# The residual stream of a two-layer decoder kept in feature-major layout: weights become the stationary operand of the second FFN product and the output projection

## The chip, the cores and the metric

The kernel runs on one core of a Trainium2 chip, as one launch. The time is device microseconds of one execution on that core. Before the change the median of three runs is 1272.65 us (1272.11 to 1273.28).

## The reference

Two layers of a decoder trunk over 256 tokens of 1024 features, all in float32. With `rms_norm` over the features, each layer does

```
x = x + 0.5 * swiglu_ffn(x, ffn1_norm, ffn1_wi, ffn1_wo)     # D_FF = 2816
h = rms_norm(x, mix_norm);  parts = split(h @ w_in)          # projections for three attentions and gates
y = g0*(o_sb @ proj_sb) + g1*(o_mla @ proj_mla) + g2*(o_nsa @ proj_nsa)
x = x + y @ w_out
x = x + 0.5 * swiglu_ffn(x, ffn2_norm, ffn2_wi, ffn2_wo)

swiglu_ffn(x, g, wi, wo): a, b = split(rms_norm(x, g) @ wi);  return (silu(a) * b) @ wo
```

The three attentions (stick-breaking, a latent one and a sparse one) are not touched by the change.

## The kernel before

Every product of float32 operands is made as three matmuls: an operand is split into a rounded part (hi) and the rest (lo), and `mm3` adds hi\*hi, hi\*lo and lo\*hi in PSUM. The weights come as a stream of slabs of 128 x 1024 (some smaller). `slab_parts` loads a slab in two halves into `raw` (six buffers, SP's queue), ScalarE (ACT) rounds a half into the hi tile and VectorE (DVE) subtracts to get the lo tile. Slabs live in one of two rings of four: `whi`/`wlo`, or `vhi`/`vlo`, which belong to the pool of a feed-forward block (FFN); `slab_tiles` chooses by the slab's number in its FFN (0 to 65). `next_slab` keeps two slabs ahead of the one in use. TensorE (PE) runs in the program's order; on the other engines a scheduler sets the order, and in the mixer (the attention part) a planner does (`Planner`, with thread after thread of `yield use_...`), for DVE and ACT as well.

The 256 tokens are two tiles of 128 (`t`), and `hq` = `hThi`/`hTlo` hold the normed input with features on the partitions, as the products need it. An FFN goes:

- Chunk 0 (slabs 0 to 3), tokens on the output's partitions: the stationary operand is a tile of `hT`, the moving one 512 columns of a slab, 48 matmuls. Its outputs are transposed by `flush` (four transposes of `g`).
- Chunks 1 to 5 (slabs 4 to 43), in `chunk_T`: the stationary operand is a 128 x 128 piece of a slab, the moving one all 256 tokens of `hq`, 24 matmuls of 256 columns for a slab. The outputs arrive with features on the partitions. `gate_T` multiplies by `rows`, the tokens' norm factors along a row; `spread_rn` makes `rows` once in an FFN by two transposes of `rnb`. The ring of a slab is v, but for slab 6 (slab 8 in the first FFN), which is w.
- The second product (slabs 44 to 65, ring w), in `out_rows`: the stationary operand is a tile of the gated values `gT` (`gh`/`gl`), the moving one 512 columns of a slab, 12 matmuls for a slab. The sums arrive with tokens on the partitions. The last three slabs (`TAIL`) are held together, so that a block of sums is finished while PE does the next.

The end of `out_rows`, for each token tile and half: the residual `x` gets the sums (L674), is multiplied by the next norm's gains (`norm`, L625, gains broadcast over the partitions by a DMA), squared and summed (`norm_scale`), transposed by PE (`half_T`, L612; in the mixer L1064) and split into `hThi` and `hTlo`. The projection `w_out` at the mixer's end is also an `out_rows`, with `yT` as the stationary operand and ring w.

In the text a slab pair of PE rows such as `acc<-hThi,vhi` names output, moving and stationary operand (moving first).

Of the kernel before, what the change touches and what calls it, by code (L numbers as in the profile page):

```python
# [10 lines left out]
F = mybir.dt.float32  # L11
# [348 lines left out]

EARLY_AT = ((27, 29, 31, 33, 35, 37, 39, 41, 43, 45), (28, 26, 32, 34, 36, 38, 40, 42, 44, 48))
# [7 lines left out]
def decoder_trunk(ctx, tc, x_in, xt_in, wts, gains, lcon, cst, out, depth=DEPTH):  # L369
# [42 lines left out]
    def load_x(t, cols=(0, 1)):  # L412
        for c in cols:
            cs = slice(c * 512, (c + 1) * 512)
            nc.sync.dma_start(xs[t][:, cs], x_in[t * 128:(t + 1) * 128, cs])

# [28 lines left out]
    nc.vector.memset(mh, -0.5)  # L445

    gain_q = []

    def load_gain():

        i = gain_n[0]
        gain_n[0] += 1
        if i < 3 * depth:
            g = cp.tile([128, D], F, tag="gain", name="gain", bufs=1)
            nc.sync.dma_start(g, gains[i:i + 1, :].to_broadcast([128, D]))
            gain_q.append(g)

    gain_n = [0]
# [148 lines left out]
    def half_T(src, half):  # L607

        tp = tp_tile()
        for j in range(4):  # L610
            k = half * 4 + j
            nc.tensor.transpose(tp[:, j * 128:(j + 1) * 128], src[:, k * 128:(k + 1) * 128], ident)  # L612
        return tp

    def to_T(dst, src, halves=(0, 1)):

        for half in halves:
            tp = half_T(src, half)
            k = slice(half * 4, half * 4 + 4)
            split(dst[0][:, k, :], dst[1][:, k, :], tp.rearrange("p (a b) -> p a b", a=4))  # L620


    def norm(h, t, c, gain):
        cs = slice(c * 512, (c + 1) * 512)
        nc.vector.tensor_tensor(h[:, cs], xs[t][:, cs], gain[:, cs], op=OP.mult)  # L625

    def norm_scale(t):

        sq = att_tile()
        ss = sm.tile([128, 16], F, tag="ss", name="ss")  # L630
        for c in range(2):
            nc.scalar.activation(sq, xs[t][:, c * 512:(c + 1) * 512], AF.Square, accum_out=ss[:, c:c + 1])
        nc.vector.tensor_scalar(ss[:, 0:1], ss[:, 0:1], ss[:, 1:2], None, op0=OP.add)
        r = rstd(ss, 1.0 / D)
        q = hp.tile([128, 8], F, tag="rn", name="rn", bufs=4)
        for i, m in enumerate((1.0, 0.5, 0.125)):
            nc.vector.tensor_scalar(q[:, i:i + 1], r[:, 0:1], m, None, op0=OP.mult)
        return q

    def enter():  # L640

        return [big_tile("h") for _ in range(NT)], new_T(), [None] * NT
# [8 lines left out]
    def out_rows(lhs, kts, between=None, last=False, by=None):  # L651
# [7 lines left out]
        for k in range(kts - TAIL):  # L659
# [4 lines left out]
            if between is not None:  # L664
                between(k)
        sls = [next_slab() for _ in range(TAIL)]
        if not last:
            gain = gain_q.pop(0)
            nxt[0] = hs, hq, rn = enter()
            hT = of_t(hq)  # L670

        def finish(t, c):
            xv = xs[t][:, c * 512:(c + 1) * 512]
            nc.vector.scalar_tensor_tensor(xv, accs[t, c], by[t][:, 1:2] if by else 0.5, xv, op0=OP.mult, op1=OP.add)  # L674
            if last:
                nc.sync.dma_start(out[t * 128:(t + 1) * 128, c * 512:(c + 1) * 512], xv)
            else:
                norm(hs[t], t, c, gain)

        tail = range(kts - TAIL, kts)  # L680
        for t in range(NT):
            cmajor = last or t == 0
            order = [(k, c) for k in tail for c in range(2)]
            if cmajor:
                order.sort(key=lambda kc: kc[1])
            for k, c in order:
                run(t, c, k, sls[k - tail[0]])
                if t == 1 and not last and c == 0 and k - tail[0] in (0, 1):
                    to_T(hT[0], hs[0], (k - tail[0],))
                if cmajor and k == kts - 1:  # L690
                    finish(t, c)
            if not cmajor:
                for c in range(2):
                    finish(t, c)
            if not last:
                rn[t] = norm_scale(t)


    def ffn(l, gi):
        first = l == 0 and gi == 0  # L700
        if first:
            nxt[0] = hs, hq, rn = enter()
            gain_n[0] = 1
        else:
            hs, hq, rn = nxt[0]
        hT = of_t(hq)
        with ExitStack() as es:
# [8 lines left out]
            gT = [(gq[0][:, :, t, :], gq[1][:, :, t, :]) for t in range(NT)]  # L716
            todo = []
            ahead = split_early(fp, l, 0) if gi == 0 else split_early(fp, l + 1, 1) if l + 1 < depth else iter(())

            def glu(t, a, b, f0, fn):  # L720
                s = fp.tile([128, 512], F, tag="gate", name="sil")
                nc.scalar.activation(s[:, :fn], a[:, :fn], AF.Silu, scale=rn[t][:, 0:1])
                g = fp.tile([128, 512], F, tag="g", name="g")
                nc.vector.tensor_tensor(g[:, :fn], b[:, :fn], s[:, :fn], op=OP.mult)
                todo.append((t, g, f0, fn))

            def flush():
                if todo:
                    t, g, f0, fn = todo.pop(0)
                    tp = tp_tile()  # L730
                    q = fn // 128
                    for j in range(q):
                        nc.tensor.transpose(tp[:, j * 128:(j + 1) * 128], g[:, j * 128:(j + 1) * 128], ident)
                    k0 = f0 // 128
                    split(gT[t][0][:, k0:k0 + q, :], gT[t][1][:, k0:k0 + q, :],
                          tp[:, :fn].rearrange("p (a b) -> p a b", a=q))

            def spread_rn():
# [7 lines left out]
                nc.scalar.activation(rows.rearrange("p t n -> p (t n)"), tp[:, 0:S], AF.Copy)  # L746

            def chunk_T(n, evac):
# [3 lines left out]
                for s in range(KT // g):  # L752
                    sl = next_slab()
                    for b, a in enumerate(accs):
# [9 lines left out]
                        if s == KT // g - 1:  # L764
                            evac(b, a)
                        yield

            def gate_T(b, a):
                if first and ci == b == 0:
                    spread_rn()  # L770
                s = fp.tile([128, 512], F, tag="gate", name="gate")
                nc.vector.tensor_tensor(s.rearrange("p (c n) -> p c n", c=2), a.rearrange("p (c n) -> p c n", c=2),
                                        rows.rearrange("p t n -> p (t n)")[:, None, :].to_broadcast([128, 2, S]),
                                        op=OP.mult)
                nc.scalar.activation(s, s, AF.Silu)
                gates[b] = s

            def value_T(b, a):
                g = fp.tile([128, 512], F, tag="g", name="g")
                nc.vector.tensor_tensor(g, a, gates[b], op=OP.mult)  # L780
# [1247 lines left out]
```

## Time and profile before

| What | Value |
|---|---|
| median of the runs | 1272.65 us |
| profiled execution, first to last instruction | 1270.3 us |
| what lies around that span, against the median | 2.35 us |
| PE / DVE / ACT / POOL busy | 1258.1 / 917.6 / 784.9 / 106.6 us |
| granted TensorE clock, mean | 0.999 |
| matmuls | 8095 |

The profile gives the span of one execution; its own device time is not listed apart, so the span is set beside the median of the runs. Busy time of PE is the union of overlapping matmuls, whose recorded durations are longer than the distance from one start to the next: for the pace of a stretch, the starts of its first and last row and the number of matmuls between them are used, not the mean duration.

The stages in that execution, by the starts of their first matmuls: FFN 1 of layer 0 from 6.30 us, its second product from 127.86, the mixer from 188.67, its `w_out` from 429.18, FFN 2 from 452.85, its second product from 575.73; layer 1 in the same order, with FFN 1 from 636.54, second product from 759.66, `w_out` from 1059.20.

### The profile page before, as it was taken

The page shows a single profiled execution, that of the slowest core. Times are in us where ns is not written, and L with a number is a line of the kernel's source. Part 1 is how long each engine was busy: PE and PEld are TensorE (multiplying, and loading weights), DVE is VectorE, ACT ScalarE, POOL GpSimd, SP SyncE. Part 2 cuts the span into 40 slices and gives each one's busy share as a digit, 9 for nine tenths or more (in the row PEclk, how much of TensorE's full clock was granted, in tenths as well). Part 3 has the DMA queues.
Part 4 walks back from the last instruction along what each step waited for, and adds up shares of the span by engine and source line. Part 5 has one row for each costly group of instructions (what it writes and reads, how often), then busy time and mean ns, then how long its engine had stood idle before and what let it go on. Part 6 is the DMA issues. An engine that isn't in the chain of part 4 may idle for free.

```text
span 1270.3 us, 23545 instructions
## 1 busy us (share of the span) xinstructions
PE 1258.1 (99%) x8095; PEld 1117.0 (88%) x8095; DVE 917.6 (72%) x1922; ACT 784.9 (62%) x1635; POOL 106.6 (8%) x169
## 2 busy tenths in 40 slices
PE   9999999999999999999999999999999999999998
PEld 8999888888877889998889998888888778899986
DVE  7777667878998676776577676678768887766643
ACT  7556557777877565565455565478757774655542
POOL 0012201110000001112000111011100000000000
PEclk9999999999999999999999999999999999999999
DMA  8789977556645567899677899674786455566653
GB/s 311 271 298 340 336 254 231 168 182 225 191 133 167 173 217 252 274 342 326 223 254 261 292 334 341 197 227 153 255 290 221 141 167 176 176 191 199 216 168 114
DMA packets 151961, 294.98 MB, mean 232 GB/s; under 512 B 17824, under 2 KB 19488, under 8 KB 151840
## 3 DMA queue, kind: packets, MB, share of 16 engines
q1 hardware_dynamic: 141984, 261.48, 63.4%
q0 software_dynamic: 9856, 31.99, 6.8%
q8 instruction: 63, 1.03, 0.3%
q14 instruction: 58, 0.48, 0.1%
HBM read 258.27 MB, written 34.60 MB: 231 GB/s over the span
## 4 chain that ended last, share of the span: by engine, by line
PE 91%; DVE 4%; ACT 2%; issue 1%; DMA 1%; POOL 0%; SPq 0%; DVEq 0%; ACTq 0%
PE acc L588 16%; PE acc L590 16%; PE acc L589 16%; PE acc L763 11%; PE acc L761 11%; PE acc L762 11%; PE tp L1562 1%; DVE x L674 1%; DMA raw<-in_wts 1%; PE att L1914 1%; PE att L1471 1%; PE tp L1590 1%; ACT wf L1521 1%; DVE wlo L536 1%; DVE vlo L536 1%
## 5 line engine op out<-in xcount | busy, mean ns | idle before, releaser
L763 PE MATMUL acc<-hThi,vlo 128*128 128x256 f32 x1248 | 344.8, 276 | 0.0
L761 PE MATMUL acc<-hThi,vhi 128*128 128x256 f32 x1248 | 344.8, 276 | 0.0
L762 PE MATMUL acc<-hTlo,vhi 128*128 128x256 f32 x1248 | 344.7, 276 | 0.0
L535 ACT ACTIVATE vhi<-raw 128x512 fp32r<-128x512 f32 x312 | 182.5, 621 | 105.3 <-PE acc L762 42.5
L536 DVE TENSOR_TENSOR vlo<-raw,vhi 128x512 fp32r<-128x512 f32 x312 | 202.9, 685 | 61.8 <-ACT vhi L535 60.1
L762 PEld LDWEIGHTS acc<-hTlo,vhi 128*128 128x128 f32 x1248 | 234.3, 188 | 0.2
L761 PEld LDWEIGHTS acc<-hThi,vhi 128*128 128x128 f32 x1248 | 234.2, 188 | 0.2
L763 PEld LDWEIGHTS acc<-hThi,vlo 128*128 128x128 f32 x1248 | 234.2, 188 | 0.0
L536 DVE TENSOR_TENSOR wlo<-raw,whi 128x512 fp32r<-128x512 f32 x248 | 160.0, 684 | 85.7 <-ACT whi L535 85.4
L535 ACT ACTIVATE whi<-raw 128x512 fp32r<-128x512 f32 x248 | 142.8, 621 | 103.8 <-PE acc L590 78.1
L588 PE MATMUL acc<-whi,hThi 128*128 128x512 f32 (+2 forms) x480 | 188.9, 394 | 0.7 <-ACT whi L535 0.7
L590 PE MATMUL acc<-whi,hTlo 128*128 128x512 f32 (+2 forms) x480 | 183.9, 383 | 0.1
L589 PE MATMUL acc<-wlo,hThi 128*128 128x512 f32 (+2 forms) x480 | 183.1, 382 | 0.2 <-DVE wlo L536 0.2
L998 DVE TENSOR_TENSOR wlo<-raw,whi 128x512 fp32r<-128x512 f32 x216 | 140.8, 678 | 25.7 <-ACT whi L996 24.5
L996 ACT ACTIVATE whi<-raw 128x512 fp32r<-128x512 f32 x216 | 126.2, 617 | 39.2 <-PE acc L590 22.8
L588 PE MATMUL acc<-whi,gh 128*128 128x512 f32 x352 | 137.5, 391 | 0.0
L590 PE MATMUL acc<-whi,gl 128*128 128x512 f32 x352 | 137.0, 389 | 0.0
L589 PE MATMUL acc<-wlo,gh 128*128 128x512 f32 x352 | 137.0, 389 | 0.0
L590 PEld LDWEIGHTS acc<-whi,hTlo 128*128 128x128 f32 x480 | 90.2, 188 | 18.8 <-DVE ss L594 1.3
L588 PEld LDWEIGHTS acc<-whi,hThi 128*128 128x128 f32 x480 | 90.4, 188 | 16.9 <-ACT whi L535 1.4
L589 PEld LDWEIGHTS acc<-wlo,hThi 128*128 128x128 f32 x480 | 90.5, 188 | 14.3 <-DVE wlo L536 0.5
L554 ACT ACTIVATE ehi<-eraw 128x512 fp32r<-128x512 f32 x60 | 37.9, 631 | 100.5 <-DMA eraw<-in_wts 99.1
(315 smaller groups left out, 1912.9 us busy)
## 6 DMA issues: line engine op xcount, KB each, us to landing
raw<-in_wts SPq DMA_DIRECT2D x764, 256.0 KB, 3.4
eraw<-in_wts SPq DMA_DIRECT2D x60, 256.0 KB, 4.8
early<-ehi POOLq DMA_DIRECT2D x60, 256.0 KB, 3.8
early<-elo POOLq DMA_DIRECT2D x60, 256.0 KB, 4.4
whi<-early SPq DMA_DIRECT2D x60, 256.0 KB, 4.0
wlo<-early SPq DMA_DIRECT2D x60, 256.0 KB, 4.1
gain<-in_gains SPq DMA_DIRECT2D x5, 512.0 KB, 5.3
xd<-x SPq DMA_DIRECT2D x4, 512.0 KB, 3.5
```

The lines of the kernel that those rows point to most:

```text
L535: nc.scalar.activation(hi[:, c:c + m], raw[:, :m], AF.Copy)
L536: nc.vector.tensor_tensor(lo[:, c:c + m], raw[:, :m], hi[:, c:c + m], op=OP.subtract)
L554: nc.scalar.activation(hi, raw, AF.Copy)
L588: nc.tensor.matmul(o, a[0], b[0], start=start, stop=False)
L589: nc.tensor.matmul(o, a[0], b[1], start=False, stop=False)
L590: nc.tensor.matmul(o, a[1], b[0], start=False, stop=stop)
L674: nc.vector.scalar_tensor_tensor(xv, accs[t, c], by[t][:, 1:2] if by else 0.5, xv, op0=OP.mult, op1=OP.add)
L761: nc.tensor.matmul(o, sl[0][:, w], h, start=k == 0 and c == 0, stop=False)
L762: nc.tensor.matmul(o, sl[0][:, w], l_, start=False, stop=False)
L763: nc.tensor.matmul(o, sl[1][:, w], h, start=False, stop=k == KT - 1 and c == 1)
L996: nc.scalar.activation(hl[0][:, c:c + m], raw[:, :m], AF.Copy)
L998: nc.vector.tensor_tensor(hl[1][:, c:c + m], raw[:, :m], hl[0][:, c:c + m], op=OP.subtract)
```

## The change

The residual is kept transposed: `xs` holds features on the partitions, tokens along the row, all the time. The rest follows.

- `out_T` takes the place of `out_rows` for three of the four second products and both `w_out`: stationary is a 128 x 128 piece of a slab, moving are all 256 tokens of `gq` or `yT`, 24 matmuls of 256 columns for a slab where there were 12 of 512. The finish of a block of 256 features (four blocks, `b`): multiply by `rows` into `u` (not for `w_out`), add to `x`, make `hThi`/`hTlo` of two feature tiles with the gain as a scalar per partition (`part_T`, ACT and DVE), square and add up (`add_squares`, ACT and DVE).
- The transposes of `h` and the broadcast gains go. All gains are one tile `gcol`. The sums of squares over the features are two float32 matmuls with a column of ones (`sum_squares`, L617), and `row_scales` makes the factors of both token tiles.
- Chunk 0 is done by a `chunk_T` too (96 matmuls of 256 columns, ring w), and the four transposes of `g` go; what needs `rows` before it is there is kept in `pend` until `spread_rn`. The square sums stand behind its third slab, in the first FFN behind the third slab of chunk 1. In the first FFN `spread_rn` moves from slab 7 to behind slab 9; slab 8 is still the one in ring w.
- The second products' slabs are in ring v, but in the last FFN. The last FFN keeps `out_rows` and so needs `x` with tokens on the partitions: `x_rows`, four times four transposes, one group in each of chunks 2 to 5.
- In the mixer `lat` takes both token tiles for each feature tile, instead of all feature tiles for each token tile, and `yT`, `V0` and `V1` have other layouts.

```diff
+    def part_T(dst, k, v, w):
+        nc.scalar.activation(dst[0][:, k], v, AF.Copy, scale=w)
+        nc.vector.scalar_tensor_tensor(dst[1][:, k], v, w, dst[0][:, k], op0=OP.mult, op1=OP.subtract)
+    def add_squares(sq, b, v):
+        nc.scalar.activation(sq[:, 512:1024] if b else sq[:, 0:512], v, AF.Square)
+        if b:
+            nc.vector.tensor_tensor(sq[:, 0:512], sq[:, 0:512], sq[:, 512:1024], op=OP.add)
+        if b == 3:
+            nc.vector.tensor_tensor(sq[:, 0:S], sq[:, 0:S], sq[:, S:2 * S], op=OP.add)
+    def sum_squares(sq):
+        a = att_tile()
+        for t in range(NT):
+            nc.tensor.matmul(a[:, t:t + 1], sq[:, t * 128:(t + 1) * 128], one, start=True, stop=True)
+        return a
...
+    def out_T(src, kts, gi, between=None, scale=None):
+        accs = [acc_tile() for _ in range(KT // 2)]
+        def run(b, k, sl):
+            h, l_ = src[0][:, k], src[1][:, k]
+            for c in range(2):
+                o = accs[b][:, c * S:(c + 1) * S].rearrange("p (t n) -> p t n", t=NT)
+                w = slice((2 * b + c) * 128, (2 * b + c + 1) * 128)
+                nc.tensor.matmul(o, sl[0][:, w], h, start=k == 0 and c == 0, stop=False)
+                nc.tensor.matmul(o, sl[0][:, w], l_, start=False, stop=False)
+                nc.tensor.matmul(o, sl[1][:, w], h, start=False, stop=k == kts - 1 and c == 1)
...
+        for b in range(KT // 2):
+            for j in range(TAIL):
+                run(b, kts - TAIL + j, sls[j])
+            xv = xs[b // 2][:, b % 2 * 512:b % 2 * 512 + 512]
+            v = accs[b]
+            if scale is not None:
+                v = scale(v)
+            nc.vector.scalar_tensor_tensor(xv, v, 0.5, xv, op0=OP.mult, op1=OP.add)
+            for k in (2 * b, 2 * b + 1):
+                part_T(hq, k, block(k), gcol[:, gi * KT + k:gi * KT + k + 1])
+            add_squares(sq, b, xv)
...
-        if not 4 <= j < FFN_SLABS - DFF // 128 or j == 6 and i != j or i == 8:
+        end = FFN_SLABS - DFF // 128 if i >= len(stream) - FFN_SLABS else FFN_SLABS
+        if not 4 <= j < end or j == 6 and i != j or i == 8:
...
+                drain(chunk_T(512, both), lambda i: scale_cols() if i == 5 else None)
...
             def hook(i):
-                if i == 3 and ci == 0 and not first:
+                if ci == 0 and first:
+                    if i == 5:
+                        scale_cols()
+                elif ci == 0 and i == 3:
                     spread_rn()
-                if i == (7 if first and ci == 0 else 3):
-                    while todo:
-                        flush()
+                if last and ci and i == 3:
+                    x_rows(ci - 1)
+                hook2(i)
+            def first_spread(i):
+                if i == 3:
+                    spread_rn()
                 hook2(i)
```

The built programs hold 8095 and 9203 matmuls. Three places show what moved. The first is PE in the first FFN, around `spread_rn` and `flush`. Before, at slab 7, after which slab 8 (ring w) follows:

```order
L763 MATMUL acc<-hThi,vlo 128x256
L733 MATMUL tp<-ident,g 128x128 x4
L761 MATMUL acc<-hThi,whi 128x256
L762 MATMUL acc<-hTlo,whi 128x256
L763 MATMUL acc<-hThi,wlo 128x256
```

Now, behind slab 9:

```order
L742 MATMUL acc<-hThi,vlo 128x256
L720 MATMUL tp<-ident,rnb 128x128 x2
L740 MATMUL acc<-hThi,vhi 128x256
L741 MATMUL acc<-hTlo,vhi 128x256
L742 MATMUL acc<-hThi,vlo 128x256
```

The transposes of `g` are gone; those of `rnb` are now followed by slabs of ring v alone, to the end of the FFN (816 matmuls with `hq`, then 528 with `gq`).

The second place is PE in chunk 0 of the FFN that follows another FFN (layer 1, FFN 1). Before, transposes of `h` stand between its matmuls:

```order
L590 MATMUL acc<-whi,hTlo 128x512
L612 MATMUL tp<-ident,h 128x128 x4
L588 MATMUL acc<-whi,hThi 128x512
L589 MATMUL acc<-wlo,hThi 128x512
L590 MATMUL acc<-whi,hTlo 128x512
```

Now the two matmuls of the square sums stand there, behind 72 of 96 matmuls:

```order
L742 MATMUL acc<-hThi,wlo 128x256
L617 MATMUL att<-gcol,sq 128x1 x2
L740 MATMUL acc<-hThi,whi 128x256
L741 MATMUL acc<-hTlo,whi 128x256
L742 MATMUL acc<-hThi,wlo 128x256
```

PE waits there for the finished sums of squares, where it waited for the residual times its gain. The third place is DVE at the same boundary. Before, these are the instructions that end with the transposed `h` in `hTlo`:

```order
L674 SCALAR_TENSOR_TENSOR x_5516<-acc_7473,rn_5759,x_5516 128x512
L536 TENSOR_TENSOR wlo_8089<-raw_8090,whi_8088 128x512
L625 TENSOR_TENSOR h_7984<-x_5516,gain_6200 128x512
L536 TENSOR_TENSOR wlo_8089<-raw_8094,whi_8088 128x512
L536 TENSOR_TENSOR vlo_8077<-raw_8098,vhi_8075 128x512
L625 TENSOR_TENSOR h_7984<-x_5516,gain_6200 128x512
```

Now, from behind the last block's residual to the last addition of squares (L611), for which PE's L617 waits (`wlo_8877` is slab 6 of the next FFN, `vlo_8726`, `vlo_8841` and `vlo_8911` are its slabs 4, 5 and 7):

```order
L609 TENSOR_TENSOR sq_8609<-sq_8609 128x512
L525 TENSOR_TENSOR wlo_8877<-raw_8878,whi_8876 128x512
L525 TENSOR_TENSOR wlo_8877<-raw_8882,whi_8876 128x512
L599 SCALAR_TENSOR_TENSOR hTlo_8608<-x_5803,gcol_106,hThi_8607 128x256 x2
L525 TENSOR_TENSOR vlo_8726<-raw_8797,vhi_8724 128x512
L525 TENSOR_TENSOR vlo_8726<-raw_8801,vhi_8724 128x512
L525 TENSOR_TENSOR vlo_8841<-raw_8842,vhi_8840 128x512
L525 TENSOR_TENSOR vlo_8841<-raw_8846,vhi_8840 128x512
L609 TENSOR_TENSOR sq_8609<-sq_8609 128x512
L525 TENSOR_TENSOR vlo_8911<-raw_8912,vhi_8910 128x512
L525 TENSOR_TENSOR vlo_8911<-raw_8916,vhi_8910 128x512
L611 TENSOR_TENSOR sq_8609<-sq_8609 128x256
```

The lo halves of four slabs, which are used after L617, stand ahead of that last addition in DVE's order.

More of the change, by code (lines that the diff above doesn't have):

```diff
@@ L410, in cc @@
         return ct[:p, o:o + w]
[L412 to L415, printed above, removed]
     def warm_up(n):
@@ L445, in decoder_trunk @@
     nc.vector.memset(mh, -0.5)
[L447 to L458, printed above, removed]
+    gcol = cp.tile([128, 128], F, name="gcol")
+    nc.vector.memset(gcol[:, NG:NG + 16], 1.0)
+    one = gcol[:, NG:NG + 1]
     lc_t = [None]
@@ L605, in of_t @@
         return [(q[0][:, :, t, :], q[1][:, :, t, :]) for t in range(NT)]
[L607 to L620, printed above, removed]
@@ L663, in out_rows @@
                     run(t, c, k, sl)
-            if between is not None:
-                between(k)
         sls = [next_slab() for _ in range(TAIL)]
[L667 to L675, printed above, removed]
-                nc.sync.dma_start(out[t * 128:(t + 1) * 128, c * 512:(c + 1) * 512], xv)
[L677 to L696, printed above, removed]
+        for t in range(NT):
+            for c in range(2):
+                for j in range(TAIL):
+                    run(t, c, kts - TAIL + j, sls[j])
+                xv = xo[t][:, c * 512:(c + 1) * 512]
+                nc.vector.scalar_tensor_tensor(xv, accs[t, c], by[t][:, 1:2], xv, op0=OP.mult, op1=OP.add)
+                nc.sync.dma_start(out[t * 128:(t + 1) * 128, c * 512:(c + 1) * 512], xv)
     def ffn(l, gi):
         first = l == 0 and gi == 0
+        last = l == depth - 1 and gi == 2
         if first:
[L702 to L706, printed above, removed]
+            nxt[0] = new_T(), big_tile("sq")
+        hq, sq = nxt[0]
         with ExitStack() as es:
@@ L715, in ffn @@
             own.append((vhi, fp.tile([128, 1024], R, tag="vlo", name="vlo", bufs=W_BUFS)))
-            gT = [(gq[0][:, :, t, :], gq[1][:, :, t, :]) for t in range(NT)]
-            todo = []
+            rn, pend = [None] * NT, []
             ahead = split_early(fp, l, 0) if gi == 0 else split_early(fp, l + 1, 1) if l + 1 < depth else iter(())
[L720 to L736, printed above, removed]
             def spread_rn():
@@ L764, in chunk_T, with soon @@
                         if s == KT // g - 1:
-                            evac(b, a)
+                            soon(evac, b, a)
                         yield
[L768 to L772, printed above, removed]
+            spread, gates = [False], {}
+            def soon(f, *a):
+                if spread[0]:
+                    f(*a)
+                else:
+                    pend.append(lambda: f(*a))
@@ L836, in first_steps @@
+                    part_T(hq, k, v, xt[:, k:k + 1])
+                parts, sl = [], []
+                accs = [acc_tile() for _ in range(2)]
                 with tc.manual_schedule(engines={nc.vector.engine, nc.scalar.engine, nc.sync.engine}):
@@ L902, in between, with scale @@
                     next(ahead, None)
-            out_rows(gT, DFF // 128, between, last=l == depth - 1 and gi == 2, by=rn)
+            if last:
+                out_rows([(gq[0][:, :, t, :], gq[1][:, :, t, :]) for t in range(NT)], DFF // 128, rn, xo)
+            else:
+                def scale(a):
+                    u = fp.tile([128, 512], F, tag="g", name="u")
+                    by_rows(u, a)
+                    return u
+                out_T(gq, DFF // 128, 3 * l + gi + 1, between, scale)
     def mixer(l):
```

239 lines of the change are left out of this document (117 added, 122 removed).

## The prediction

> **What bounds the kernel now.** I read the page from the top: the busy times, the clock, the chain that ended last.
>
> ```profile
> PE 1258.1 (99%) x8095; PEld 1117.0 (88%) x8095; DVE 917.6 (72%) x1922; ACT 784.9 (62%) x1635; POOL 106.6 (8%) x169
> PEclk9999999999999999999999999999999999999999
> PE 91%; DVE 4%; ACT 2%; issue 1%; DMA 1%; POOL 0%; SPq 0%; DVEq 0%; ACTq 0%
> L763 PE MATMUL acc<-hThi,vlo 128*128 128x256 f32 x1248 | 344.8, 276 | 0.0
> L588 PE MATMUL acc<-whi,gh 128*128 128x512 f32 x352 | 137.5, 391 | 0.0
> ```
>
> TensorE bounds everything, at full clock in every slice; only some tens of us are waits. So the question is how long PE takes for the matmuls as they are now cut, and whether it waits at the new seams. The mean durations (276 and 391 ns) overlap and would mislead: two of 256 columns are not 552 ns. The pace comes from the starts in the timeline of PE.
>
> ```profile
> 127.86 0.40 PE L588 MATMUL acc<-whi,gh 128*128 128x512 f32 x1
> 184.33 0.60 PE L612 MATMUL tp<-ident,h 128*128 128x128 f32 x4
> ...
> 17.81 0.28 PE L761 MATMUL acc<-hThi,vhi 128*128 128x256 f32 x1
> 27.71 0.38 PE L745 MATMUL tp<-ident,rnb 128*128 128x128 f32 x2
> 27.84 0.36 PE L761 MATMUL acc<-hThi,vhi 128*128 128x256 f32 x1
> 28.05 0.28 PE L762 MATMUL acc<-hTlo,vhi 128*128 128x256 f32 x1
> 29.35 0.60 PE L733 MATMUL tp<-ident,g 128*128 128x128 f32 x4
> 29.70 0.36 PE L761 MATMUL acc<-hThi,whi 128*128 128x256 f32 x1
> 29.90 0.28 PE L762 MATMUL acc<-hTlo,whi 128*128 128x256 f32 x1
> 32.66 0.28 PE L761 MATMUL acc<-hThi,vhi 128*128 128x256 f32 x1
> ...
> 465.90 0.28 PE L761 MATMUL acc<-hThi,vhi 128*128 128x256 f32 x1
> 471.56 0.38 PE L745 MATMUL tp<-ident,rnb 128*128 128x128 f32 x2
> ```
>
> - 512 columns: 249 matmuls from 127.86 to 184.33, 226.8 ns each.
> - 256 columns with weights in ring w: 23 from 29.90 to 32.66, 120.0 ns.
> - 256 columns with weights in ring v: 840 from 32.66 to 127.86, 113.3 ns. But the same kind took 84 from 17.81 to 27.71, 117.9 ns, and 11 from 28.05 to 29.35, 118.2 ns.
>
> So ring v has two paces. The slow one stands after a start from 512-column matmuls (17.81) and after a start from transposes (28.05); the fast one stands only behind slab 8, which is in ring w (29.70). The other three FFNs repeat it, slow before their slab in ring w (48 from 465.90 to 471.56, 117.9 ns) and fast behind it. In the built program `whi` and `wlo` start a multiple of 512 bytes from the `hT` tiles, `vhi` 192 bytes off such a multiple; the changed program has the same distances, and sets `gh` to `vhi` and `yT` to `whi` 192 off as well.
>
> **The change, part by part.** T is the end of a product on PE. The seams before, and the lat stage:
>
> ```profile
> 6.30 0.50 PE L588 MATMUL acc<-whi,hThi 128*128 128x512 f32 x1 [0.71 <-ACT whi L535]
> ...
> 184.69 0.48 PE L588 MATMUL acc<-whi,gh 128*128 128x512 f32 x1
> 186.16 0.60 PE L612 MATMUL tp<-ident,h 128*128 128x128 f32 x4
> 193.57 0.45 PE L588 MATMUL acc<-whi,hThi 128*128 128x440 f32 x1
> 199.69 0.40 PE L588 MATMUL acc<-whi,hThi 128*128 128x512 f32 x1
> 429.18 0.39 PE L588 MATMUL acc<-whi,yT 128*128 128x512 f32 x1
> 475.09 0.28 PE L761 MATMUL acc<-hThi,vhi 128*128 128x256 f32 x1
> 575.73 0.40 PE L588 MATMUL acc<-whi,gh 128*128 128x512 f32 x1
> 640.34 0.65 PE L612 MATMUL tp<-ident,h 128*128 128x128 f32 x4 [0.91 <-DVE h L625]
> 659.02 0.28 PE L761 MATMUL acc<-hThi,vhi 128*128 128x256 f32 x1
> 759.66 0.40 PE L588 MATMUL acc<-whi,gh 128*128 128x512 f32 x1
> 831.51 0.39 PE L588 MATMUL acc<-whi,hThi 128*128 128x512 f32 x1
> ```
>
> Prices. The change splits 1176 matmuls of 512 into pairs of 256 (3 x 264 in second products, 2 x 96 in `w_out`, 4 x 48 in chunk 0). At the fast pace a pair costs 2 x 113.3 = 226.6 ns: nothing; at the slow one 9 ns more, in ring w with `hT` 13 more. A group of four transposes costs 0.36 us (184.33 to 184.69), and the six matmuls behind it 1.47 us (to 186.16) instead of 1.36: 0.47. Two `rnb` transposes with the restart: 0.3. The float32 square sums (two of one column) appear nowhere; below, two transposes (0.22 us), above, a group of four twice over (0.94); I take 0.5 with the restart, nearer to the transposes because the weights loaded are the same 128 x 128. The lat matmuls take 204 ns (30 from 193.57 to 199.69).
>
> The Trainium skill ("TensorE: Matmul & The Clock Gate", section "Back-to-back issue gap") puts N/2.4 + 2.5 ns on a warm matmul, so 2.5 ns for each of the 1176 that are added: 2.9 us against the change. The trace differs: 256 columns take exactly half of 512 at the fast pace, so no such term stands in the sum.
>
> What DVE must do at a seam:
>
> ```profile
> 639.00 0.68 DVE L536 TENSOR_TENSOR wlo<-raw,whi 128x512 fp32r<-128x512 f32 x1
> 639.60 0.68 DVE L625 TENSOR_TENSOR h<-x,gain 128x512 f32<-128x512 f32 x1
> 640.20 0.68 DVE L536 TENSOR_TENSOR wlo<-raw,whi 128x512 fp32r<-128x512 f32 x1
> ...
> L772 DVE TENSOR_TENSOR gate<-acc,rows 128x512 f32<-128x512 f32 x40 | 27.2, 685 | 9.5 <-PE acc L763 9.5
> L833 DVE SCALAR_TENSOR_TENSOR hTlo<-h,xt,hThi 128x256 fp32r<-128x256 f32 x6 | 2.9, 478 | 0.0
> raw<-in_wts SPq DMA_DIRECT2D x764, 256.0 KB, 3.4
> ```
>
> Back to back, 512 elements cost DVE 0.60 us; 256 elements then cost about 0.39 (478 ns less the same overlap of 85). By the order of the changed kernel, from the first block's sums to the last addition of squares:
> - FFN to FFN: 20 of 512 (4 `u`, 4 residuals, 3 additions, 9 half slabs), 8 `hTlo`, one short addition: 12.0 + 3.1 + 0.3 = 15.4 us. PE allows three blocks of 18 (6.12) and 72 in ring w (8.64), 14.8 us. So PE waits 0.7 us at least; since slab 7 loads into the `raw` buffer that slab 4 frees late (3.4 us to landing), up to 3.5. I take 2.0. Queued behind that wait are slab 3's matmuls and all that follows.
> - `w_out` to FFN: 18 of 512 (no `u`, 11 half slabs): 14.2 us against 6.4 + 8.6. Nothing to 1.5; I take 0.5.
> - FFN to mixer: 14 of 512: 11.8 us against 6.1 + 36 x 0.204 = 13.5. No wait; `lat` by feature tile needs the last ones only at T + 7.3.
>
> The tiles themselves come in time: the last `hTlo` pair stands eight DVE instructions ahead of L611, and is needed by slab 3.
>
> The sum against the trace, with the slow pace after each restart into ring v (us, now minus before):
> 1. First FFN to slab 8, 26.36 (6.30 to 32.66): chunk 0 96 x 0.120 + 0.63 of waits as before, slabs 4 to 6 at the fast pace since they follow ring w 8.16, square sums 0.5, slab 7 2.83, slab 8 2.88: 26.5, +0.2.
> 2. Slabs 9 to 43, 95.20: slab 9 2.72, `rnb` 0.3, then 816 x 0.1179 = 96.2: +4.0. No slab of ring w follows the transposes any more.
> 3. Second product and lat, 71.83 (127.86 to 199.69): 528 x 0.1179 + 48 x 0.204 + 0.6: 72.6, +0.8. (The 16 transposes removed are paid away by the pace.)
> 4. `w_out` to slab 6, twice 45.91 (429.18 to 475.09): 192 x 0.1179, two groups of `y` 0.94, chunk 0 11.52, square sums and wait 1.0, slabs 4 and 5 5.44, `rnb` 0.3, slab 6 2.88: 44.7, -2.4 for both.
> 5. FFN to FFN, 83.29 (575.73 to 659.02), fast since slab 6 is in ring w behind `rnb`: 59.8 + 11.5 + 0.5 + 2.0 + 5.4 + 0.3 + 2.9 = 82.5, -0.8.
> 6. Layer 1 FFN to mixer, 71.85: 59.8 + 9.8 + 0.6 = 70.2, -1.6.
> 7. Last FFN: four groups `x_rows` 1.9, and from the first on 720 matmuls slow (720 x 4.6 ns = 3.3): +5.2.
>
> Together +5.3 before rounding: 1275.6 against the span of 1270.3, and with the 2.35 us around it, as in the median, 1278.0. Costed at nothing: the gain broadcasts that go and the residual's new DMAs (under PE work with two slabs ready); ACT's share of `part_T`, which is shorter than DVE's; the new order at the mixer's start, where only a few groups change places. If that cover is gone, the late one is DVE's weight split, since it already ends waits at these seams.
>
> **Rivals.**
> - *The fast pace holds.* If a restart does not bring the slow pace back, 816 + 528 + 384 + 720 = 2448 matmuls lose their 4.6 ns: 11.3 us less, 1266.7, faster. For it: nowhere before is a fast stretch interrupted, so that it is lost has not been seen. Against it: five clean starts into ring v all ran slow. It decides at a mean pace of 115.7 ns over these 2448. The Trainium skill (same page, "Step-by-step: what each phase is for") says "Loading the next tile's weights doesn't steal SBUF read bandwidth from the running matmul"; by that all should run alike, as here. The trace disagrees already, with 113.3, 117.9 and 120.0 ns for one shape.
> - *Slow only beside `hT`.* If the pace recovers with `gh` or `yT` as moving tile (no row has them), terms 3 and 4 lose 4.2: 1273.8.
> - *DVE is later than counted.* With 3.5 us and twice 1.5 of waits, and a row of `raw` loads behind them: 1281.5. For it: 0.91 us of waiting for DVE at 640.34 already, with less queued. Against it: 640.34 is DVE work that PE needs at once, the new tiles have 5 to 7 us.
>
> **Chances.** Slow pace after restarts 0.50, fast pace 0.27, slow beside `hT` alone 0.15, late DVE 0.08. A change under 0.2% (2.5 us) can't be told from none here. Faster is the second case and a little of the third, 0.29; the same, most of the third and the edge of the first, 0.16; slower 0.55. The range 1266 to 1282 takes in the second and the last case; the first alone has 1275 to 1281.
>
> **What would show it.** In the timeline after: `acc<-gh,vhi` of layer 0's FFN 1 at 118 ns and of its FFN 2 at 113; chunk 0 at 120; a wait of PE at L617 with DVE as releaser, longest between the layers; no row L612 of `h`; DVE not above 75%. The prediction is wrong if the paces of those two second products are equal, or if PE waits several us in the mixer.

## The result, and the profile after

The changed kernel takes 1286.13 us (median of 4 executions, 1284.61 to 1287.78), the kernel before beside it 1272.97 us (1272.11 to 1273.41): 1.0102 times as long, 95% interval 1.0088 to 1.0116. It is slower by 13 us, where 5 were forecast; 1286 lies above the range of 1266 to 1282. The profiled execution spans 1284.4 us against 1270.3.

The page of the changed kernel: busy times, the granted clock in 40 slices, the chain that ended last, the two largest groups of 256 columns, and the weight transfers.

```profile
PE 1266.3 (99%) x9215; PEld 1174.9 (91%) x9215; DVE 928.2 (72%) x1924; ACT 790.1 (62%) x1627; POOL 104.7 (8%) x164
PEclk9999999999999999999989999999999999999999
PE 85%; DVE 5%; ACT 4%; DMA 2%; issue 2%; POOL 0%; SPq 0%; DVEq 0%; ACTq 0%
L740 PE MATMUL acc<-hThi,vhi 128*128 128x256 f32 x1248 | 346.9, 278 | 0.0
L647 PE MATMUL acc<-gh,vhi 128*128 128x256 f32 x528 | 146.3, 277 | 0.0
raw<-in_wts SPq DMA_DIRECT2D x764, 256.0 KB, 3.3
```

Three things are new. PE has 1108 matmuls more (the trace lists each of the 12 of the square sums as two rows, so 9215 stand there for 9203) and is still "busy" 99%: a busy share hides both a slower pace and a slower clock. One digit of the clock is an 8, in the slice from 642 to 674 us. And the chain has lost 6 points from PE to the other engines. The largest waits of PE inside the layers, with the releaser, total, times and longest, say to whom:

```profile
PE att L617 <- DVE sq L611: 8.9, 5, 3.7
...
PE tp L1665 <- DMA zc<-wf: 1.3, 1, 1.3
PE tp L1545 <- ACT wf L1536: 1.1, 3, 0.6
```

The first row is the wait that the change adds: PE at the square sums (L617), for DVE's last addition of squares (L611), once at each of five seams. The longest is between the layers. PE's timeline there, with the two second products of layer 0 for their pace:

```profile
130.67 0.28 PE L647 MATMUL acc<-gh,vhi 128*128 128x256 f32 x1
...
192.86 0.36 PE L577 MATMUL acc<-whi,hThi 128*128 128x440 f32 x1
...
580.97 0.28 PE L647 MATMUL acc<-gh,vhi 128*128 128x256 f32 x1
...
640.81 0.28 PE L740 MATMUL acc<-hThi,whi 128*128 128x256 f32 x1
...
649.33 0.28 PE L742 MATMUL acc<-hThi,wlo 128*128 128x256 f32 x1
653.29 0.99 PE L617 MATMUL att<-gcol,sq 128*128 128x1 f32 x4 [3.68 <-DVE sq L611]
654.14 0.56 PE L740 MATMUL acc<-hThi,whi 128*128 128x256 f32 x1
...
659.40 0.41 PE L740 MATMUL acc<-hThi,vhi 128*128 128x256 f32 x1
...
659.97 0.28 PE L740 MATMUL acc<-hThi,vhi 128*128 128x256 f32 x1
```

- 528 matmuls from 130.67 to 192.86: 117.8 ns each. 528 of the same form from 580.97 to 640.81: 113.3 ns. The two paces are there, as forecast.
- Chunk 0 runs its first 72 matmuls at 120 ns, then PE stands for 3.7 us, and then slab 3's 24 matmuls take from 654.14 to 659.40: 219 ns each.

That last number is no wait. The same stretch by windows (the stretch and its length, the busy time of PE, its weight loads, DVE, ACT and POOL, then the granted clock, the DMA engines' share and GB/s) shows the clock at half:

```profile
652.00:654.00 2.00, 0.71 (x4) 0.74 (x4) 1.75 (x4) 0.85 (x3) 0.00 (x0) 0.76 0.92 242
654.00:656.00 2.00, 2.00 (x11) 2.00 (x11) 0.76 (x2) 0.50 (x1) 0.56 (x1) 0.50 0.90 298
...
658.00:660.00 2.00, 2.00 (x12) 2.00 (x12) 1.21 (x6) 0.10 (x1) 1.12 (x2) 0.54 0.43 166
660.00:662.00 2.00, 2.00 (x20) 2.00 (x19) 0.00 (x0) 0.00 (x0) 0.00 (x0) 1.00 0.46 170
```

A wait of 3.7 us thus cost 6.7: itself, and 3.0 at a clock of 0.50 behind it (27 matmuls in 5.83 us instead of 3.23, and the sums in 0.85 instead of 0.44). Why DVE was so late is in its own timeline, with one row of ACT's ahead of it:

```profile
636.18 1.25 ACT L524 ACTIVATE whi<-raw 128x512 fp32r<-128x512 f32 x2 [1.37 <-DMA raw<-in_wts]
...
636.85 0.69 DVE L525 TENSOR_TENSOR wlo<-raw,whi 128x512 fp32r<-128x512 f32 x1 [1.31 <-ACT whi L524]
637.46 0.68 DVE L756 TENSOR_TENSOR u<-acc,rows 128x512 f32<-128x512 f32 x1
...
643.91 0.69 DVE L756 TENSOR_TENSOR u<-acc,rows 128x512 f32<-128x512 f32 x1
...
652.73 0.42 DVE L611 TENSOR_TENSOR sq<-sq 128x256 f32<-128x256 f32 x1
```

The first block's sums were complete at about 634.7 (640.81 less 54 matmuls of 113.3 ns). `u`, which needs them, started at 637.46: ahead of it in DVE's queue stood the split of a chunk-0 weight slab, and DVE was idle for 1.31 us for that slab's `whi`, for which ACT had been idle for 1.37 us until its transfer landed. From there to the end of L611 DVE took 15.7 us.

The whole difference of the two traces by the prediction's steps, in us (now minus before):

| stretch | forecast | measured |
|---|---|---|
| start to first matmul | 0 | -1.3 |
| 1. first FFN to slab 8 | +0.2 | +0.1 |
| 2. slabs 9 to 43 | +4.0 | +4.0 |
| 3. second product, lat | +0.8 | +1.7 |
| 4. `w_out` to slab 6, twice | -2.4 | -1.0 |
| 5. FFN to FFN | -0.8 | +4.1 |
| 6. layer 1 FFN to mixer | -1.6 | 0.0 |
| 7. last FFN | +5.2 | +5.0 |
| the two mixers behind lat | 0 | +2.0 |
| last second product | 0 | -0.5 |
| sum | +5.3 | +14.1 |

### The profile page after: what moved, and what is told of

Read it like the earlier page. It is cut to its first block, busy times and chain, and to the rows that moved or that the text cites. A ratio compares the mean times of both kernels' runs of the same rounds, so it can differ in the third digit from the quotient of the medians.

```text
span 1284.4 us, 25746 instructions
## 1 busy us (share of the span) xinstructions
PE 1266.3 (99%) x9215; PEld 1174.9 (91%) x9215; DVE 928.2 (72%) x1924; ACT 790.1 (62%) x1627; POOL 104.7 (8%) x164
## 4 chain that ended last, share of the span: by engine, by line
PE 85%; DVE 5%; ACT 4%; DMA 2%; issue 2%; POOL 0%; SPq 0%; DVEq 0%; ACTq 0%
PE acc L740 12%; PE acc L742 12%; PE acc L741 12%; PE acc L577 9%; PE acc L579 9%; PE acc L578 9%; PE acc L647 5%; PE acc L648 5%; PE acc L649 5%; DMA raw<-in_wts 2%; PE tp L1545 1%; DVE wlo L982 1%; ACT whi L980 1%; DVE hTlo L599 1%; ACT wf L1504 1%
## 5 line engine op out<-in xcount | busy, mean ns | idle before, releaser
L525 DVE TENSOR_TENSOR vlo<-raw,vhi 128x512 fp32r<-128x512 f32 x444 | 288.0, 687 | 107.0 <-ACT vhi L524 106.4
L524 ACT ACTIVATE vhi<-raw 128x512 fp32r<-128x512 f32 x444 | 258.2, 622 | 156.7 <-PE acc L741 53.5
L982 DVE TENSOR_TENSOR wlo<-raw,whi 128x512 fp32r<-128x512 f32 x216 | 141.3, 679 | 21.3 <-ACT whi L980 20.1
L980 ACT ACTIVATE whi<-raw 128x512 fp32r<-128x512 f32 x216 | 126.3, 617 | 43.1 <-PE acc L579 23.3
L649 PE MATMUL acc<-gh,vlo 128*128 128x256 f32 x528 | 146.4, 277 | 0.0
L647 PE MATMUL acc<-gh,vhi 128*128 128x256 f32 x528 | 146.3, 277 | 0.0
L648 PE MATMUL acc<-gl,vhi 128*128 128x256 f32 x528 | 146.3, 277 | 0.0
L525 DVE TENSOR_TENSOR wlo<-raw,whi 128x512 fp32r<-128x512 f32 x116 | 75.5, 684 | 44.0 <-ACT whi L524 43.7
L524 ACT ACTIVATE whi<-raw 128x512 fp32r<-128x512 f32 x116 | 68.0, 621 | 58.6 <-PE acc L579 26.4
L544 DVE TENSOR_TENSOR elo<-eraw,ehi 128x512 fp32r<-128x512 f32 x60 | 41.5, 692 | 84.1 <-ACT ehi L543 84.1
L648 PEld LDWEIGHTS acc<-gl,vhi 128*128 128x128 f32 x528 | 99.2, 188 | 0.0
L649 PEld LDWEIGHTS acc<-gh,vlo 128*128 128x128 f32 x528 | 99.1, 188 | 0.0
```

What stands on the lines that cost most here:

```text
L524: nc.scalar.activation(hi[:, c:c + m], raw[:, :m], AF.Copy)
L525: nc.vector.tensor_tensor(lo[:, c:c + m], raw[:, :m], hi[:, c:c + m], op=OP.subtract)
L647: nc.tensor.matmul(o, sl[0][:, w], h, start=k == 0 and c == 0, stop=False)
L648: nc.tensor.matmul(o, sl[0][:, w], l_, start=False, stop=False)
L649: nc.tensor.matmul(o, sl[1][:, w], h, start=False, stop=k == kts - 1 and c == 1)
L982: nc.vector.tensor_tensor(hl[1][:, c:c + m], raw[:, :m], hl[0][:, c:c + m], op=OP.subtract)
```

## The experiments

Theory: two paces of ring v, decided at each start of the matmul stream, and sums that PE asks for before DVE has them, with the clock's drop behind the wait. Twelve kernels tell the parts apart. Times are medians in us; the ratio is to the kernel before, run beside each group of them, whose median was 1272.97 for the first row and 1273.36, 1273.12, 1272.44 and 1272.95 for the others. So times of two rows may differ by up to 1 us for that alone.

| kernel | time | range | ratio (95%) |
|---|---|---|---|
| changed | 1286.13 | 1284.61 to 1287.78 | 1.0102 (1.0088 to 1.0116) |
| slab 10 in ring w | 1285.44 | 1278.99 to 1287.42 | 1.0081 (1.0061 to 1.0100) |
| ring w behind `x_rows` | 1285.63 | 1282.64 to 1286.23 | 1.0092 (1.0079 to 1.0105) |
| wait filled with matmuls | 1283.99 | 1282.74 to 1287.01 | 1.0087 (1.0074 to 1.0100) |
| late sums, three FFNs | 1279.91 | 1277.49 to 1281.28 | 1.0051 (1.0039 to 1.0063) |
| late sums, mixers too | 1275.61 | 1274.64 to 1277.67 | 1.0021 (1.0012 to 1.0029) |
| the same and ring w behind `x_rows` | 1272.54 | 1271.64 to 1275.59 | 1.0004 (0.9995 to 1.0013) |
| and slab 10 (all three edits) | 1272.74 | 1267.31 to 1276.03 | 0.9988 (0.9975 to 1.0001) |
| before, slab 8 in ring v | 1276.14 | 1275.43 to 1278.62 | 1.0023 (1.0013 to 1.0033) |
| `gh` moved by 192 bytes | 1293.54 | 1291.48 to 1294.38 | 1.0155 (1.0142 to 1.0168) |
| all three, no early slabs in the first FFN | 1279.80 | 1278.16 to 1280.65 | 1.0056 (1.0043 to 1.0069) |
| all three, six early slabs | 1280.21 | 1278.09 to 1286.21 | 1.0069 (1.0051 to 1.0086) |
| all three, early slabs spread | 1272.26 | 1264.65 to 1276.10 | 0.9987 (0.9975 to 1.0000) |

### The waits and the clock

**The wait filled.** In `scale_cols`, in the FFN between the layers only:

```
+                if l and not gi:
+                    z = att_tile()
+                    for _ in range(17):
+                        nc.tensor.matmul(z, hq[0][:, 0, 0, :], hq[0][:, 0:2], start=True, stop=True)
                 rn[:] = row_scales(sum_squares(sq))
```

> The changed kernel, with 17 matmuls of 512 columns (17 x 0.227 = 3.85 us, into a PSUM tile that nobody reads) ahead of the square sums between the layers, so that PE is busy while it waits there. Theory of the clock: it is the 3.7 us of idleness that halves the granted clock, so slab 3 runs at 120 instead of 219 ns and the first matmuls of slab 4 at full pace: -2.4 and -0.4, the added matmuls cost what the wait did (+0.1 to 0.3): 1283.5. Rival, slab 3 is slow because its operands come late: it stays at about 219 ns and the time at 1286 or, with the added work, up to 1286.5.

PE's timeline at that seam:

```profile
649.59 4.04 PE L781 MATMUL att<-hThi 128*128 128x512 f32 x17
653.47 0.50 PE L617 MATMUL att<-gcol,sq 128*128 128x1 f32 x4
653.83 0.37 PE L740 MATMUL acc<-hThi,whi 128*128 128x256 f32 x1
...
656.80 0.28 PE L740 MATMUL acc<-hThi,vhi 128*128 128x256 f32 x1
```

The sums start no earlier than in the changed kernel (653.47 against 653.29), but slab 3's 24 matmuls take 2.97 us, 124 ns each, instead of 219: idleness it was that cost the clock. The median fell by 2.1 us of 2.6 expected. The profiled execution, though, was the longest of the four (mean clock 0.997, the others 0.999 to 1.000): there the clock dropped at two other seams, behind waits of 1.8 and 1.4 us; the second of them:

```profile
PE att L617 <- DVE sq L611: 1.4, 1, 1.4
```

```profile
1102.00:1104.00 2.00, 2.00 (x12) 2.00 (x13) 1.51 (x5) 0.89 (x3) 0.48 (x1) 0.61 0.89 321
1104.00:1106.00 2.00, 2.00 (x12) 2.00 (x11) 1.72 (x7) 0.62 (x1) 0.22 (x1) 0.54 0.88 298
```

In the changed kernel's own trace the four waits of 1.1 to 1.7 us left the clock at 1.00. So a wait of this length drops it in some executions and not in others. The kernels below say how little decides: in the last of them (early slabs spread) two waits of 0.9 and 0.5 us, one behind the other at the seam between the layers, dropped it (first row), and with late sums everywhere waits of 1.0 and 0.4 us at the same seam did not (second row). With `gh` moved, a wait of 2.6 us there left it at 1.00 too.

```profile
656.00:658.00 2.00, 2.00 (x11) 2.00 (x11) 1.21 (x6) 0.33 (x1) 1.12 (x2) 0.50 0.79 305
```

```profile
656.00:658.00 2.00, 2.00 (x20) 2.00 (x19) 2.00 (x8) 1.15 (x2) 1.13 (x2) 1.00 0.70 263
```

Each drop in these traces, but for the idle end of the kernel, lasted 3.4 us or twice that, as the 6.8 us behind the wait of 3.7. The Trainium skill ("TensorE: Matmul & The Clock Gate", section "What's actually happening") describes a free-running activity window of about 3.4 us behind whose idleness the clock is halved; these lengths, and that the same wait does and does not trip it, fit such a window. Not in agreement is how much idleness it takes: the page has a whole idle window, and its summary no idle gaps over about 3 us, which is too generous for this kernel: 1.4 us was enough, and 0.9 and 0.5 together.

**Late sums.** In three FFNs the sums go behind slab 3 instead of slab 2; in a second kernel also the mixers' sums, by a due time in the planner:

```
-                drain(chunk_T(512, both), lambda i: scale_cols() if i == 5 else None)
+                drain(chunk_T(512, both), lambda i: scale_cols() if i == 7 else None)
...
-            k = yield "P", 0.4, 0.6, (Tok(7.0),), (s_tp,)
+            k = yield "P", 0.4, 0.6, (Tok(9.5),), (s_tp,)
```

> The changed kernel, with the square sums of chunk 0 issued after slab 3 instead of after slab 2, in the three FFNs that wait there. Theory (the sums come too early for DVE): 24 matmuls more, 2.9 us, go ahead of the wait; of 3.7 us between the layers 0.8 are left, the clock stays up (-2.4), and the two waits behind w_out (1.2 us each) vanish: -7.7 us, 1278.4, if the rnb transposes behind slab 5 still find their rows ready. Rival, DVE's lateness is only handed on: the rnb transposes wait for the scales instead (4.2 us from the sums to rnb, 5.4 of PE work between), PE loses there what it gains here: 1283 to 1286.

> The changed kernel with late sums in three FFNs as before, and in the two mixers after 9.5 us of its plan instead of 7.0. Theory: the waits of 1.1 and 1.7 us at the mixers' start vanish, and with them the clock's drop that a run sometimes shows there (up to 1.5 us): -2.8 to -4 from the 1279.9 of late sums alone: 1276 to 1277. Rival, the low-rank branch of the mixer waits for the scales and its products come later: 1280 or more.

PE's waits for DVE's squares, first with the FFNs' sums late, then with all:

```profile
PE att L617 <- DVE sq L611: 2.9, 3, 1.5
```

```profile
PE att L617 <- DVE sq L611: 1.0, 1, 1.0
```

8.9 us in five waits become 2.9 in three and 1.0 in one; the time goes to 1279.9 and 1275.6, the mean clock of the profiled executions from 0.997 to 1.000. Little waits in DVE's place: the `rnb` transposes find their rows ready, and a wait of 0.4 us for a slab's transfer behind the sums between the layers is new. Both expectations held within 1.5 us. The waits and what the clock adds to them are 10.5 of the 13 us; without all but 1.0 us of them the change costs 2.5 us.

### The paces

**The kernel before without its slab in ring w.** Nothing but `or i == 8` taken out of `slab_tiles`.

> The kernel before, with its slab 8 of the first FFN in ring v like its neighbours, and nothing else. Pace theory: no ring-w slab follows the transposes, the 840 matmuls behind it keep 117.9 ns: +3.9 us, slab 8 itself -0.05: 1277.1 against 1273.3. Rival, the pace of 113.3 comes by itself once the first transfers are over: no change, 1273.3.

```profile
29.46 0.36 PE L761 MATMUL acc<-hThi,vhi 128*128 128x256 f32 x1
...
131.31 0.40 PE L588 MATMUL acc<-whi,gh 128*128 128x512 f32 x1
```

864 matmuls in 101.85 us, 117.9 ns, where the kernel before has 98.16: +3.7 in this stretch, +3.0 in the median. A kernel in which the change does not exist loses the same pace in the same way.

**Ring w behind `x_rows`**, in the last FFN:

```
-        if not 4 <= j < end or j == 6 and i != j or i == 8:
+        if i >= len(stream) - FFN_SLABS and j in (14, 22, 30, 38) or not 4 <= j < end or j == 6 and i != j or i == 8:
```

> The changed kernel, with slabs 14, 22, 30 and 38 of the last FFN in ring w, each right behind a group of x_rows transposes. Pace theory: 96 matmuls at 120 instead of 118.2 ns, +0.2 us, the other 624 behind the first group at 113.3 instead of 118.2, -3.1: -2.9 us, 1283.2. Rival, the slow pace stands beside the copies of xo and lasts whatever slab comes next: +0.2 us, 1286.3; and if ring w's slots come free too late for these slabs, PE waits for them and it is slower than 1286.5.

From slab 7 to the end of the chunks this stretch takes 103.03 us instead of 105.60, 2.6 less; the 168 matmuls (120 at the end) behind each slab of ring w run at 113.3 ns. The median moved by 0.5 only, 0.9 against the kernels before beside them, under the scatter that the clock's drops bring (1282.64 to 1286.23). Once the waits are gone the same edit shows in the time: 1275.61 to 1272.54, and against the kernels before beside them from +2.5 to +0.1.

> The kernel with all three edits but with slab 8, not slab 10, of the first FFN in ring w, as in the changed kernel: late sums at five seams and the last FFN's ring-w slabs alone. If the two edits add up: 1275.6 less 2.6, 1273.0, level with before, and with less spread than all three edits (1267 to 1276), since nothing in the first FFN depends on a hiccup. Rival, the edits disturb one another: 1275 or more.

It came out at 1272.54, level with before.

**`gh` moved.** `gh` starts at 16 instead of 96 elements of four bytes in its tile (320 bytes lower, which up to a multiple of 512 is 192 higher), `gl` at 48 instead of 0 (192 bytes higher); no instruction differs.

> The changed kernel, with gh and gl moved by 192 bytes within their tiles, so that vhi starts a multiple of 512 bytes from them (vlo 256 off); no instruction changes. Theory of the distance (a weight tile a multiple of 512 bytes away costs 120.0 ns): the 1056 matmuls of the second products of layer 0's FFN 2 and layer 1's FFN 1 go from 113.3 to 118 or 120 ns, those 528 of the first FFN from 117.8 to 118 to 120: +4.7 us if only the two of three with vhi slow down, +8.2 if all do: 1291 to 1294.5. Rival, the distance does not matter and the rings differ by something else: no change, 1286.

```profile
583.08 0.28 PE L647 MATMUL acc<-gh,vhi 128*128 128x256 f32 x1
...
646.43 0.28 PE L740 MATMUL acc<-hThi,whi 128*128 128x256 f32 x1
```

528 matmuls in 63.35 us: 120.0 ns, in all three second products, whatever the pace was ahead of them. That makes these products 8.2 us longer in the trace, and the time 7.4 us. All 528 are slow, also the third whose weights are `vlo`, 256 bytes off; whether that distance is slow by itself or the other two thirds hold it back is not told apart. One `vhi` is fast with `gh` at one place and slow at the other, and one `hT` is slow with `whi` and not with `vhi`: so it is not the place of one tile but where the two lie to one another that sets the pace. That the 120.0 ns of ring w with `hT` is the same thing is inferred from the equal distance and the equal pace; no run moved those tiles, and no other distances were tried.

### The first FFN

**Slab 10 in ring w**, behind `rnb` (`i == 10` for `i == 8`):

> The changed kernel, with the first FFN's one later slab in ring w moved from slab 8 to slab 10, right behind the two rnb transposes. Pace theory: the restart now leads into a ring-w slab, so ring v behind it runs at 113.3 ns: 33 slabs of 24 and the 528 of the second product, 1320 matmuls, lose 4.6 ns each; slab 10 itself costs 2 ns more, slab 8 2 less: -6.0 us, 1280.1 against 1286.1. Rival, the pace belongs to this stretch of the program (first FFN, other transfers under way) and not to what follows a restart: no change, 1286, still 118 ns behind rnb.

PE's timeline in the first FFN:

```profile
37.54 0.28 PE L740 MATMUL acc<-hThi,vhi 128*128 128x256 f32 x1
...
114.89 0.28 PE L741 MATMUL acc<-hTlo,vhi 128*128 128x256 f32 x1
115.29 0.39 PE L742 MATMUL acc<-hThi,vlo 128*128 128x256 f32 x1
115.52 0.28 PE L740 MATMUL acc<-hThi,vhi 128*128 128x256 f32 x1
...
128.59 0.28 PE L647 MATMUL acc<-gh,vhi 128*128 128x256 f32 x1
```

Neither theory alone: ring v does run at 113.3 ns behind the slab, until the stream stops for 0.3 us at 114.89, and from there on at 117.8 to the end of the second product. The pace is decided again at a stop, also one of a few tenths of a us, and either way: in the same trace a stop of 0.1 us at 48.65 had begun the slow pace and the next, at 51.47, the fast one. What PE stopped for at 114.89 is the lo half of a weight, and why that was late stands in the rows of ACT and DVE:

```profile
111.47 0.63 ACT L543 ACTIVATE ehi<-eraw 128x512 fp32r<-128x512 f32 x1 [3.11 <-DMA eraw<-in_wts]
...
112.14 0.69 DVE L544 TENSOR_TENSOR elo<-eraw,ehi 128x512 fp32r<-128x512 f32 x1 [2.37 <-ACT ehi L543]
...
114.55 0.69 DVE L525 TENSOR_TENSOR vlo<-raw,vhi 128x512 fp32r<-128x512 f32 x1
```

`eraw` is half a slab that is split ahead for the mixer. Its transfer was late, both engines stood idle for it, and the split of the weight that PE needed next stood behind it in their queues: once it had come they had no further idle time before 114.55. It is what happened at the seam between the layers, where a weight split stood ahead of `u`. The stop at 183.83 in the second product is another kind: there ACT was idle for 2.47 us for the weight's own transfer. And because PE was earlier, it waited 2.96 us for the squares at the mixer, with the clock dropping there. So 0.7 us of the 6 came out in the median (1.1 against the kernels before beside them), and single executions range over 8 us.

**All three edits**: late sums at five seams, ring w behind `x_rows`, slab 10.

> The changed kernel with the sums later at all five seams that waited (after slab 3 in three FFNs; in the mixers after 9.5 us of its plan instead of 7.0), the last FFN's four ring-w slabs behind x_rows, and the first FFN's ring-w slab behind rnb. Theory (slow pace and early sums are the whole loss): from the 1279.9 of late sums alone -2.6 for the last FFN, -2.8 for the mixers' waits, -2.3 to -6.0 for the first FFN as far as its fast pace survives the late weights there: 1268.5 to 1272, level with before (1273) or faster. Rival, at the fast pace the first FFN runs into its weight transfers and PE waits there, and later scales delay the mixer: 1275 to 1278.

1272.74 lies 0.7 us above the theory's range and below the rival's. Of the twelve executions one is below that range (1267.31), four are in it and seven above. Whether late weights are what decides between them is told by taking the early slabs away (`ahead = iter(())` in the first FFN):

> The kernel with all three edits, whose first FFN splits no slabs ahead for its mixer (the 20 half slabs, 256 KB in and 512 KB out each, are left out there and loaded by the mixer itself). Theory (the first FFN loses its fast pace to weights that come late because the DMA engines are busy, 0.90 to 0.97 of their time from 90 to 170 us): behind rnb 792 + 528 matmuls run at 113.3 ns with no hiccup, 149.6 us from slab 11 to the end of the second product against 154.1 with all three edits and 158.4 in the changed kernel; the mixer pays with 20 splits more on DVE and ACT, so the total says little: 1268 to 1280. Rival, the pace there has another cause, the residual's copies or gh as moving tile: still 117.8 ns in the second product, 152 us or more.

```profile
38.00 0.28 PE L740 MATMUL acc<-hThi,vhi 128*128 128x256 f32 x1
...
127.76 0.28 PE L647 MATMUL acc<-gh,vhi 128*128 128x256 f32 x1
...
187.60 0.36 PE L577 MATMUL acc<-whi,hThi 128*128 128x440 f32 x1
```

```profile
90.00:170.00 80.00, 80.00 (x708) 80.00 (x707) 45.59 (x72) 38.57 (x68) 0.00 (x0) 1.00 0.63 197
```

1320 matmuls in 149.60 us, 113.3 ns each, with no stop, as expected to the tenth; the DMA engines are busy 0.63 of the time. (The 158.4 us of the changed kernel in that expectation count slab 10 as well; from slab 11 on it is 155.5.) In the kernel that keeps slab 8 and the early slabs (1272.54 us) it is 0.96:

```profile
90.00:170.00 80.00, 80.00 (x681) 80.00 (x680) 54.36 (x87) 44.79 (x81) 15.18 (x28) 1.00 0.96 330
```

That kernel has no stop in this stretch either, at the slow pace, so busy DMA engines alone do not stop PE. The edit takes away two things at once, the transfers and the early slabs' splits from the queues of ACT and DVE, and no run tells which of them gives the steady pace. The mixer pays more than is won: 1279.8. Two attempts to keep both failed.

> The kernel with all three edits, with six slabs instead of ten split ahead in the first FFN, so that its second product has the DMA engines to itself. Theory of the late weights: the second product keeps the fast pace in most executions, 2.4 us and the late weights' 0.5 to 1 less: 1269 to 1271, faster than before by 0.2 to 0.3%, if the mixer has room for four splits more. Rival, DVE and ACT lack the time in the mixer: 1273 or more.

With the first list of `EARLY_AT` cut to six slabs the first FFN does keep its pace (the same 149.60 us), but the first mixer waits for DVE, and the time is 1280.2, a miss of 10 us. The edit does more than the expectation says: FFN 1 of layer 1 takes the same list, so its mixer too has four slabs fewer ready (44 early half slabs in the trace for 60). The longest wait is in the first mixer, and the clock was at half for 6.8 us, from shortly before that wait's end:

```profile
PE tp L1545 <- DVE su L1870: 3.9, 1, 3.9
```

> The kernel with all three edits, with the first FFN's 20 half slabs for its mixer spread more evenly: two more steps in its third chunk, two fewer in its second product, whose last slabs then load with no such step between. The same bytes, all steps kept. Theory of the late weights: fewer executions lose the fast pace in the second product (2.4 us) and the late weights at its end go (0.5 to 1 us): median 1270 to 1271.5, 0.1 to 0.2% below before, with less spread than 1267 to 1276. Rival, the load of the DMA engines where steps stand every second slab is what makes a weight late, wherever it stands: 1272 to 1274, as with all three edits.

Spread over more of the first FFN (`ci >= 2` for `ci >= 3`, and `k % 5 in (1, 3)` for `k % 2`), the same transfers give 1272.26. The rival held: the profiled execution lost the pace at 92.41 to a weight half that came 0.4 us late, again behind an early half slab for whose transfer ACT was idle (5.12 us), and the range of executions grew to 1264.65 to 1276.10. No version's median here is below the kernel before by more than 0.2%, and none of the intervals lies wholly below 1.

## Why the prediction was wrong in size

- **Steps 1, 2 and 7, the pace: right**, within 0.3 us each. Slow behind `rnb` and behind `x_rows`, 113 ns behind slab 6, chunk 0 at 120, and no price for splitting a matmul in two: the 528 of 256 columns between the layers take 113.3 ns, half of the 226.8 of one of 512. The 2.5 ns for each matmul that the Trainium skill ("TensorE: Matmul & The Clock Gate", "Back-to-back issue gap") would have added appear nowhere; the section gives them for an isolated matmul, not for a stream that loads weights for each, as this one does.
- **Step 5, the wait for L617: the step that failed.** I took 2.0 us, with 3.5 as its upper end; it was 3.7, and in the profiled execution the clock's drop added 3.0 behind it. DVE's work was counted rightly, 15.4 us against 15.7. Wrong was where the count begins: I let DVE start when the first block's sums are complete, but its queue is in order, and a weight split that waited for its own transfer stood ahead of `u` (2.8 us).
- **Steps 3 and 6: "No wait" was wrong by the same omission.** At the last seam `u` started at 825.30, 2.6 us behind its sums, and PE waited 1.7 us; at the first mixer 1.1.
- **Step 4: 0.5 us taken for the wait, 1.3 and 1.2 measured.** Here DVE started on time, 0.2 us behind the first block's sums, but took 16.1 us where I counted 14.2. Its work was 14.9, and twice it was idle for 0.58 us, for ACT's `hThi`, with the next residual behind that in its queue; ACT's share of `part_T` was costed at nothing. PE finishes a block's sums only every 2.1 us there, so DVE would have waited for them instead if ACT had been faster (an estimate from the same rows). A total of DVE's work from the first block on leaves both out.
- **Not in the sum at all:** a price for idleness beyond the idle time. The granted clock was 1.00 before until PE's last matmul, so nothing in that profile showed it. The rival of a late DVE was right in kind, but had a chance of 0.08, waits of 6.5 us in sum, none of them at a mixer, where 8.9 were measured, and nothing for the clock, so its 1281.5 was too low as well. With all but 1.0 us of the waits taken away the change costs 2.5 us, and the forecast less its 3.0 us of waits was +2.3. That these agree so closely is luck in part: three stretches set at nothing came out at -1.3, +2.0 and -0.5 us and nearly cancel.
- **The fast-pace rival** was wrong, and its condition, that a restart does not bring back the slow pace, was refuted in both kernels. So was the rival of a slow pace beside `hT` alone: `gh` ran at 117.8 ns in the first FFN and `yT` at 118.4.
- **The signs named beforehand** all came true, the paces, the wait at L617 and its releaser. They tested the mechanisms, and none of them the size of the wait.
- **Not explained:** the two mixers' +2.0 us. They are spread over many small gaps; no experiment was made on them alone.

## What to carry to other kernels

When a step makes the bounding engine wait for another, do not compare amounts of work; write down the helper's queue in order, with what each item ahead itself waits for, and ask for the result later rather than exactly on time. Fill or shorten every wait of TensorE of more than about a microsecond, since in these traces the clock charged some of them again. And before splitting or transposing matmuls, measure the pace from their starts, for each pair of buffers and behind each kind of start: here one shape had three paces, 6% apart, and the middle one instead of the fast one took 11.3 us from the change (816 + 528 + 384 + 720 matmuls at 4.6 ns).

## What the runs showed of the hardware

- One shape of matmul (128 x 128 weights, 256 columns) has three paces at full clock: 113.3, 117.9 and 120.0 ns. With the weight tile a multiple of 512 bytes from the moving tile it was 120.0 wherever these kernels had it, and moving one tile so that it stood there changed 113.3 to 120.0.
- The two others are states of the stream: which one holds is decided at a start or a stop, also a stop of 0.1 us, and stays for hundreds of matmuls. Why, was not found.
- The clock dropped to 0.50 for 6.8 us behind a wait of 3.7 us, and for 3.4 us behind waits of 1.8 and 1.4 us and of 0.9 and 0.5 us together; in other executions waits of 2.6 and 1.7 us left it at 1.00.
- Filling a wait with matmuls that nobody reads keeps the clock up: 124 instead of 219 ns behind the same wait.
